# Start of a decoder layer on one core: x loaded by tokens with its squares summed along rows, the first unit's products in float32, and another order of the first two blocks

## The chip, the cores and the metric

One of the eight cores of a Trainium2 chip runs the whole layer. The metric is the device time of one execution in microseconds (us); lower is better. The engines are PE (TensorE, matmuls), ACT (ScalarE), DVE (VectorE), POOL (GpSimd) and SP (SyncE, which here only issues DMA transfers). Each takes its instructions in the order in which the program lists them.

## What is computed

A decoder layer over 256 tokens of width 2048, all in float32. Cut to the part that this case touches:

```python
mod = silu(c) @ w_ada[l] + b_ada[l]                       # 6 vectors of 2048: shifts, scales, gates
sh1, sc1, gt1, sh2, sc2, gt2 = split(mod, 6)
h = rmsnorm(x, g_pre_mix[l]) * (1.0 + sc1) + sh1          # x is 256 x 2048
proj = h @ w_in[l]                                        # q, k, v of two attentions, an indexer, two gates
# ... two attentions, gated merge, output projection, MLP of width 8192, residuals
```

## The kernel before

**Tiles.** Features are cut into KT = 16 blocks of P = 128, tokens into NT = 2 halves, the columns of `w_in` into chunks of CW = 512. `xt` holds x by features: `xt[:, k]` is block k, 128 features by 256 tokens.

**Products.** A float32 product is made of three faster ones. ACT casts a piece of the weight w to its high part wh (line 269, up to 1024 columns at a time), DVE subtracts it from w to get the low part wl (line 270), h is split in the same way, and PE adds hi·wh, hi·wl and lo·wh (lines 284 to 286). A *unit* is the work on one chunk of columns for a few blocks: `dk1[0:3]` is the second chunk of one attention's keys, blocks 0 to 2. Its two PSUM banks, one per token half, are ps0a and ps1a, or ps0b and ps1b in turn. When the unit ends they are *evicted* into an accumulator in SBUF such as `p_dk1`: by an ACT copy (line 527) the first time, by a DVE add (line 529) for ps0 later, while ps1 is refilled from the accumulator by a copy (line 315) ahead of its unit and copied out again.

**The sweep.** h of block k needs `sc[k]` and `sh[k]`, each the dot product of 128 rows of `w_ada` (1 MB) with silu(c): one DVE instruction over 2048 columns (`ada_item`, line 466). So the kernel sweeps over the blocks: the planner `sweep()` lists loads of `w_ada` ("sc k", "sh k") and units over the blocks that are there already, in an order from estimated loading and working times. `items` is that list; every item has a `load` (a DMA issue on SP into one of four buffers "w"), a `split` (casts and subtractions, or the dot) and perhaps an `mm` (products and evictions). The loop at the end of the program issues loads and splits some items ahead of the products; a scheduler then sets the order of ACT's and DVE's instructions, save where a stretch stands under `manual_schedule`, which keeps the order of the code. The first FIRST = 2 blocks come as "sc", "sh" and one unit `first_products` over four chunks (EARLY: two of the indexer's queries, mq0, mk0); their eight banks stay open over both blocks.

**The start.** `start()` loads silu's argument, the identity and xT in four transfers, makes `cB` (silu(c) along every partition), squares x by features and adds the squares over partitions with matmuls against a column of ones (`pss`), takes the root of the mean and spreads its inverse into `rx`, keeps PE busy with `keep_warm` (matmuls whose result nobody reads), and does the dots, h (`h_block`) and weight splits of block 0. In this kernel DVE alone is under manual order there.

## Time and profile before

| | |
|---|---|
| median of 3 runs | 1473.7 us (1473.13 to 1476.2) |
| the profiled execution's own time | 1474.31 us |
| its span in the profile | 1472.5 us |
| PE busy | 1449.0 us, 98% |
| DVE busy | 1049.1 us, 71% |
| ACT busy | 772.8 us, 52% |
| moved by DMA | 371.60 MB, mean 252 GB/s |

The span is what the profiler saw from first to last instruction; some 2 us lie around it. Busy shares are means over the whole span: whether an engine bounds a stretch is read from the waits of that stretch. The profile gives TensorE's granted clock as a share of full speed.

### The profile page before, as it was taken

To read this page: it belongs to the slowest core of one execution; us is meant where nothing else is said; L and a number is where in the kernel's file an instruction comes from. 1 tells how busy PE (TensorE), PEld (TensorE's weight loads), DVE (VectorE), ACT (ScalarE), POOL (GpSimd) and SP (SyncE) were. 2 spreads that over 40 slices of the span, in tenths; PEclk is the share of its full clock that TensorE was granted. 3 is DMA by queue.
4 is the path that set the end of the run, shared out by engine and by line. 5 is a ranking of instruction groups with operands and counts; after the bars stand their busy time and mean duration, and the time that the engine had idled before them with its cause. 6 is when DMAs were issued, how large, how long until landed. Compare 5 with 4: busy or idle time off the path is not lost.

```text
span 1472.5 us, 18227 instructions
## 1 busy us (share of the span) xinstructions
PE 1449.0 (98%) x7042; PEld 1214.0 (82%) x7042; DVE 1049.1 (71%) x1317; ACT 772.8 (52%) x1113; POOL 5.7 (0%) x14
## 2 busy tenths in 40 slices
PE   7999999999999999999999999999999999999997
PEld 6877788778888888888888888888888888888886
DVE  6799887999876777987587665677655655565555
ACT  4676776667685454444474444444434443344443
POOL 0000000000000000000000000000000000000000
PEclk9999999999999999999999999999999999999999
DMA  8999996475879899878526666756765545555551
GB/s 315 325 330 333 343 343 245 177 280 207 335 274 327 332 347 335 321 290 312 233 95 250 256 234 252 257 218 240 257 243 190 196 177 195 200 198 176 198 189 68
DMA packets 56150, 371.60 MB, mean 252 GB/s; under 512 B 6464, under 2 KB 6624, under 8 KB 15616
## 3 DMA queue, kind: packets, MB, share of 16 engines
q1 hardware_dynamic: 55152, 367.98, 68.3%
q0 software_dynamic: 704, 2.18, 0.5%
q8 instruction: 55, 0.90, 0.2%
q10 hardware_dynamic: 208, 0.28, 0.1%
q14 instruction: 31, 0.25, 0.1%
HBM read 368.30 MB, written 2.11 MB: 252 GB/s over the span
## 4 chain that ended last, share of the span: by engine, by line
PE 92%; DVE 4%; ACT 1%; issue 1%; DVEq 0%; ACTq 0%
PE ps L286 16%; PE ps L285 16%; PE ps L284 16%; PE ps L365 16%; PE ps L367 8%; PE ps0b L285 1%; PE ps0b L284 1%; PE ps0b L286 1%; PE ps1b L285 1%; PE ps0a L284 1%; PE ps1b L286 1%; PE ps0a L285 1%; DVE wl L270 1%; PE ps1b L284 1%; PE ps0a L286 1%; PE ps1a L286 1%
## 5 line engine op out<-in xcount | busy, mean ns | idle before, releaser
L270 DVE TENSOR_TENSOR wl<-w,wh 128x1024 fp32r<-128x1024 f32 (+1 forms) x472 | 562.7, 1202 | 333.4 <-ACT wh L269 324.8
L269 ACT CAST wh<-w 128x1024 fp32r<-128x1024 f32 (+1 forms) x472 | 486.8, 1035 | 552.5 <-PE ps L286 336.3
L365 PE MATMUL ps<-h,wh 128*128 128x512 f32 (+1 forms) x1056 | 257.1, 386 | 0.0
L466 DVE SCALAR_TENSOR_TENSOR w<-w,cB 128x2048 f32<-128x2048 f32 x96 | 219.3, 2285 | 29.5 <-DMA w<-in_ada 29.3
L365 PEld LDWEIGHTS ps<-h,wh 128*128 128x128 f32 x1056 | 186.8, 189 | 32.1
L284 PE MATMUL ps<-wh,f 128*128 128x512 f32 x512 | 199.3, 389 | 0.0
L285 PE MATMUL ps<-wl,f 128*128 128x512 f32 x512 | 199.2, 389 | 0.0
L286 PE MATMUL ps<-wh,f 128*128 128x512 f32 x512 | 199.2, 389 | 0.0
L367 PEld LDWEIGHTS ps<-h,wl 128*128 128x128 f32 x1024 | 139.5, 190 | 9.7
L367 PE MATMUL ps<-h,wl 128*128 128x256 f32 x1024 | 142.8, 282 | 0.0
L284 PE MATMUL ps<-wh,h 128*128 128x512 f32 x320 | 126.8, 396 | 0.0
L285 PE MATMUL ps<-wl,h 128*128 128x512 f32 x320 | 124.9, 390 | 0.0
L286 PE MATMUL ps<-wh,h 128*128 128x512 f32 x320 | 124.9, 390 | 0.0
L284 PEld LDWEIGHTS ps<-wh,f 128*128 128x128 f32 x512 | 96.1, 188 | 20.0
L286 PEld LDWEIGHTS ps<-wh,f 128*128 128x128 f32 x512 | 96.1, 188 | 20.0
L285 PEld LDWEIGHTS ps<-wl,f 128*128 128x128 f32 x512 | 96.1, 188 | 19.8
L286 PEld LDWEIGHTS ps<-wh,h 128*128 128x128 f32 x320 | 60.1, 188 | 12.7
L284 PEld LDWEIGHTS ps<-wh,h 128*128 128x128 f32 x320 | 60.1, 188 | 12.2 <-issue 0.3
L285 PEld LDWEIGHTS ps<-wl,h 128*128 128x128 f32 x320 | 60.2, 188 | 11.9
L284 PE MATMUL ps<-wh,o 128*128 128x512 f32 x128 | 50.1, 391 | 0.0
L286 PE MATMUL ps<-wh,o 128*128 128x512 f32 x128 | 49.8, 389 | 0.0
L285 PE MATMUL ps<-wl,o 128*128 128x512 f32 x128 | 49.8, 389 | 0.0
(326 smaller groups left out, 1791.6 us busy)
## 6 DMA issues: line engine op xcount, KB each, us to landing
w<-in_w_ff SPq DMA_DIRECT2D x128, 1024.0 KB, 4.8
w<-in_ada SPq DMA_DIRECT2D x96, 1024.0 KB, 6.0
w<-in_w_in SPq DMA_DIRECT2D x60, 1024.0 KB, 6.3
w<-in_w_in SPq DMA_DIRECT2D x27, 768.0 KB, 6.0
w<-in_w_o SPq DMA_DIRECT2D x16, 1024.0 KB, 5.7
w<-in_w_moba SPq DMA_DIRECT2D x8, 1024.0 KB, 7.1
w<-in_w_dsa SPq DMA_DIRECT2D x8, 1024.0 KB, 7.1
w<-in_w_in SPq DMA_DIRECT2D x14, 512.0 KB, 4.8
```

The lines of the kernel that those rows point to most:

```text
L269: yield (lambda h=h, src=src: S.copy(h, src), lambda h=h, l=l, src=src: V.tensor_tensor(l, src, h.bitcast(F32), ALU.subtract))
L270: lambda h=h, l=l, src=src: V.tensor_tensor(l, src, h.bitcast(F32), ALU.subtract))
L284: TE.matmul(ps[t][:, :cw], hi, h, start=f, stop=False, skip_group_check=skip)
L285: TE.matmul(ps[t][:, :cw], hi, l, start=False, stop=False, skip_group_check=skip)
L286: TE.matmul(ps[t][:, :cw], lo, h, start=False, stop=e, skip_group_check=skip)
L365: TE.matmul(out, w, acts()[:, k, :, ts], start=k == 0 and ts.start == 0, stop=False)
L367: TE.matmul(out[:, 0], w, acts()[:, k, 0, ts], start=False, stop=k == KT - 1)
L466: V.scalar_tensor_tensor(w, w, 1.0, cB, ALU.mult, ALU.mult, accum_out=mod[:, i:i + 1])
```

## The change

x comes in by tokens first (four transfers of 512 KB into the tile that held the squares), and ACT squares each part with a running sum along its row (`accum_out`), so that the sums over features come out directly; the DVE adds and the matmuls with ones are gone. cs and con are loaded from ACT's queue. xT is still needed and is loaded in pieces: blocks 0 and 1 in the start, blocks 2 and 3 after the first six items, then four blocks at a time, six items ahead of sh 4, sh 8 and sh 12. Unit 0's products are float32 matmuls of h (written over `xt[:, 0]`) with the raw weights, without cast or subtraction. The new `h_first` takes the place of `h_block` for blocks 0 and 1; block 1's high part is made before its float32 copy, and unit 1 goes hi·wh, lo·wh, hi·wl over its four chunks in the order 2, 3, 0, 1, with the evictions inside. One warm-up matmul more; all of `start()` is in manual order on ACT too and covers the first six items.

```diff
@@ -397,7 +397,7 @@
 
     xt = pre.tile([P, KT, T], F32, name="xt")
     spare = pre.tile([P, 4, 2 * CW], F32R, name="spare")
-    sq = act.tile([P, KT, T], F32, name="sq", tag="act")
+    sq = act.tile([P, NT * D], F32, name="sq", tag="act")
...
-        nc.sync.dma_start(cs[:, 0], cT)
-        nc.sync.dma_start(con[:, :P], consts[:, :P])
-        for h in range(4):
-            nc.sync.dma_start(xt[:, 4 * h:4 * h + 4], xT[:, 4 * h:4 * h + 4])
+        nc.scalar.dma_start(cs[:, 0], cT)
+        nc.scalar.dma_start(con[:, :P], consts[:, :P])
+        xs = [(t, h, sq[:, (2 * t + h) * D // 2:(2 * t + h + 1) * D // 2]) for t in range(NT) for h in range(2)]
+        for t, h, part in xs:
+            nc.sync.dma_start(part, x[t * P:(t + 1) * P, h * D // 2:(h + 1) * D // 2])
+        items[0]["load"]()
+        nc.sync.dma_start(xt[:, :FIRST], xT[:, :FIRST])
+        for it in items[1:4]:
+            it["load"]()
         nc.gpsimd.dma_start(b_sb, bT)
         nc.gpsimd.dma_start(g_sb, gT)
         S.activation(cs[:, 1], cs[:, 0], AF.Sigmoid)
         V.tensor_tensor(cs[:, 0], cs[:, 0], cs[:, 1], ALU.mult)
         sqrt_table(cs[:, 1, 0:1])
-        for n in range(NC):
-            S.copy(cB[:, n * CW:(n + 1) * CW], rows(cs[:, 0, 4 * n:4 * n + 4], ("tp", "sc")[n % 2]))
-        for it in items[:4]:
-            it["load"]()
-        pss = [bank(tag, "pss") for tag in ("tp", "sc")]
-        for h in range(4):
-            s4 = sq[:, 4 * h:4 * h + 4]
-            S.activation(s4, xt[:, 4 * h:4 * h + 4], AF.Square)
-            V.tensor_tensor(s4[:, 0:2], s4[:, 0:2], s4[:, 2:4], ALU.add)
-            if h == 3:
-                V.tensor_tensor(s4[:, 0:1], s4[:, 0:1], s4[:, 1:2], ALU.add)
-            n = 1 if h == 3 else 2
-            for i in range(n):
-                for t in range(NT):
-                    TE.matmul(pss[t][:, 0:1], s4[:, i, t * P:(t + 1) * P], ones[:, 0:1],
-                              start=h == 0 and i == 0, stop=h == 3)
         V.tensor_scalar(g_sb, g_sb, -0.5, None, ALU.mult)
         for sec in (1, 4):
             V.tensor_scalar(b_sb[:, sec * KT:(sec + 1) * KT], b_sb[:, sec * KT:(sec + 1) * KT], 1.0, None, ALU.add)
+        ssx = sm.tile([P, NT, 2], F32, name="ssx", tag="ssx", bufs=1)
+        for n, (t, h, part) in enumerate(xs):
+            S.copy(cB[:, n * CW:(n + 1) * CW], rows(cs[:, 0, 4 * n:4 * n + 4], ("tp", "sc")[n % 2]))
+            S.activation(part, part, AF.Square, accum_out=ssx[:, t, h:h + 1])
         a, rc, q, m = (sm.tile([P, NT], F32, name=f"x{i}", tag=f"x{i}", bufs=1) for i in "arqm")
-        items[0]["split"]()
-        for t in range(NT):
-            V.tensor_copy(m[:, t:t + 1], pss[t][:, 0:1])
-        root = rsqrt_mean(rc, a, m, q)
-        run(root)
+        V.tensor_tensor(m, ssx[:, :, 0], ssx[:, :, 1], ALU.add)
+        run(rsqrt_mean(rc, a, m, q))
         S.copy(rx, rows(rc, "sc")[:, :T])
-        keep_warm(rx, 4)
-        items[1]["split"]()
-        first = list(items[2]["halves"]())
-        h0 = h_block(0)
-        next(h0)
-        for high, low in first:
-            high()
-            low()
-        next(h0, None)
+        keep_warm(rx, 5)
+        for k in range(FIRST):
+            scale, shift, unit = items[3 * k:3 * k + 3]
+            if k:
+                shift["load"]()
+            scale["split"]()
+            h = h_first(k)
+            next(h)
+            if k:
+                unit["load"]()
+            shift["split"]()
+            next(h)
+            parts = list(unit["halves"]())[::-1] if k else ()
+            for high, _ in parts:
+                high()
+            next(h, None)
+            for _, low in parts:
+                low()
+            if not k:
+                unit["mm"]()
+                unit["mm"] = lambda: None
...
+    def h_first(k):
+
+        sc, sh = s1[:, 0, k:k + 1], s1[:, 1, k:k + 1]
+        i = KT + k
+        V.scalar_tensor_tensor(sc, mod[:, i:i + 1], b_sb[:, i:i + 1], g_sb[:, 0, k:k + 1], ALU.add, ALU.mult)
+        hf = tmpt("hf")[:, :T]
+        V.scalar_tensor_tensor(hf, xt[:, k], sc, rx, ALU.mult, ALU.mult)
+        yield
+        V.tensor_tensor(sh, mod[:, k:k + 1], b_sb[:, k:k + 1], ALU.add)
+        dst = xt[:, k], h1[:, k, 0]
+        S.activation(dst[k > 0], hf, AF.Identity, bias=sh)
+        yield
+        S.activation(dst[k == 0], hf, AF.Identity, bias=sh)
+        V.scalar_tensor_tensor(h1[:, k, 1], hf, sh, h1[:, k, 0].bitcast(F32), ALU.add, ALU.subtract)
+
     def h_block(k):
-
         sc, sh = s1[:, 0, k:k + 1], s1[:, 1, k:k + 1]
         i = KT + k
         V.scalar_tensor_tensor(sc, mod[:, i:i + 1], b_sb[:, i:i + 1], g_sb[:, 0, k:k + 1], ALU.add, ALU.mult)
@@ -493,7 +509,6 @@
         V.scalar_tensor_tensor(hf, xt[:, k], sc, rx, ALU.mult, ALU.mult)
         S.activation(h1[:, k, 0], hf, AF.Identity, bias=sh)
         V.scalar_tensor_tensor(h1[:, k, 1], hf, sh, h1[:, k, 0].bitcast(F32), ALU.add, ALU.subtract)
-        yield
         S.activation(xt[:, k], hf, AF.Identity, bias=sh)
...
     def first_products(off, k):
 
+
         it = {}
 
         def mm():
-            for i, name in enumerate(EARLY):
-                if k == 0:
+            if k == 0:
+                for i, name in enumerate(EARLY):
                     opened[name] = hold(name) if name in IQ else pair(True)
-                else:
-                    products(opened[name], h1, k, it["parts"][i:i + 1], CW, (), (), range(NT), True)
-                if k == FIRST - 1:
                     for t in range(NT):
-                        evict(name, True, False, t, opened[name][t])
-            for p, q in ((0, 0), (1, 0), (0, 1)) if k == 0 else ():
-                for i, name in enumerate(EARLY):
+                        TE.matmul(opened[name][t], xt[:, 0, t * P:(t + 1) * P], it["w"][:, i * CW:(i + 1) * CW],
+                                  start=True, stop=False, skip_group_check=True)
+                return
+            for p, q in ((0, 0), (1, 0), (0, 1)):
+                for i in (2, 3, 0, 1):
+                    name = EARLY[i]
                     for t in range(NT):
-                        TE.matmul(opened[name][t], h1[:, 0, p, t * P:(t + 1) * P], it["parts"][i][q],
-                                  start=p == q == 0, stop=False, skip_group_check=True)
-        it.update(load=lambda: load(it, w_in, off, 4 * CW), split=lambda: split(it, CW, 4),
+                        TE.matmul(opened[name][t], h1[:, k, p, t * P:(t + 1) * P], it["parts"][i][q],
+                                  start=False, stop=k == FIRST - 1 and q == 1, skip_group_check=True)
+                        if q:
+                            evict(name, True, False, t, opened[name][t])
+        it.update(load=lambda: load(it, w_in, off, 4 * CW), split=lambda: None,
                   halves=lambda: halves(it, CW, 4), mm=mm)
...
-            items.append(ada_item(0, k0, (lambda k=k0: run(h_block(k))) if k0 else None))
+            if k0 % 4 == 0 and k0:
+                items.insert(len(items) - 6, dict(load=lambda k=k0: nc.sync.dma_start(xt[:, k:k + 4], xT[:, k:k + 4]),
+                                                  split=lambda: None, mm=None))
+            items.append(ada_item(0, k0, (lambda k=k0: h_block(k)) if k0 >= FIRST else None))
...
-    items.insert(24, dict(load=lambda: nc.sync.dma_start(con[:, P:], consts[:, P:]), split=lambda: None, mm=None))
+    items.insert(3 * FIRST, dict(load=lambda: nc.sync.dma_start(xt[:, FIRST:4], xT[:, FIRST:4]), split=lambda: None, mm=None))
+    items.insert(26, dict(load=lambda: nc.sync.dma_start(con[:, P:], consts[:, P:]), split=lambda: None, mm=None))
...
-    with tc.manual_schedule(engines={mybir.EngineType.DVE}):
+    with tc.manual_schedule(engines={mybir.EngineType.DVE, mybir.EngineType.Activation}):
         start()
-    loads, splits = 4, 3
+    loads = splits = 3 * FIRST
```

The scheduler's order on ACT and DVE is another one from the start to some 180 rows of ACT further on; from there the two programs agree. Three places follow. Numbers behind names tell buffers of one name apart.

ACT around dk1[0:3], which runs right after dq1[0:3], before (spare and wh of w_440 are the casts of dk1[0:3]; p_dq1 is the eviction of the unit ahead of it; h1_90 and xt_81 are h of a block of features):

```order
L491 ACTIVATE s1_91<-mod_89,b_sb_85 128x1
L269 CAST spare_82<-w_440 128x1024
L494 ACTIVATE h1_90<-hf_475,s1_91 128x256
L497 ACTIVATE xt_81<-hf_475,s1_91 128x256
L269 CAST spare_82<-w_440 128x512
L269 CAST wh_508<-w_470 128x1024
L527 COPY p_dq1_100<-ps0b_244 128x512
L527 COPY p_dq1_100<-ps1b_245 128x512
```

and in the changed kernel, where dk1[0:3]'s weights are w_427:

```order
L507 ACTIVATE s1_91<-mod_89,b_sb_85 128x1
L510 ACTIVATE h1_90<-hf_432,s1_91 128x256
L512 ACTIVATE xt_81<-hf_432,s1_91 128x256
L542 COPY p_dq1_100<-ps0b_205 128x512
L269 CAST spare_82<-w_427 128x1024
L542 COPY p_dq1_100<-ps1b_206 128x512
L269 CAST spare_82<-w_427 128x512
L269 CAST wh_467<-w_437 128x1024
```

The eviction of dq1's first bank has moved ahead of dk1's first cast, and that of its second bank ahead of the second.

ACT around mq1[4:7], which runs right after mk0[4:7], before (wh of w_918 are mq1's casts, p_mk0<-ps1a the eviction of mk0's second bank):

```order
L527 COPY p_mq0_92<-ps1b_245 128x512
L315 COPY ps1b_245<-p_mq1_94 128x512
L269 CAST wh_959<-w_918 128x1024
L491 ACTIVATE s1_91<-mod_89,b_sb_85 128x1
L269 CAST wh_963<-w_918 128x512
L494 ACTIVATE h1_90<-hf_952,s1_91 128x256
L497 ACTIVATE xt_81<-hf_952,s1_91 128x256
L527 COPY p_mk0_93<-ps1a_243 128x512
```

and in the changed kernel, where the weights are w_905:

```order
L542 COPY p_mq0_92<-ps1b_206 128x512
L315 COPY ps1b_206<-p_mq1_94 128x512
L542 COPY p_mk0_93<-ps1a_204 128x512
L507 ACTIVATE s1_91<-mod_89,b_sb_85 128x1
L269 CAST wh_940<-w_905 128x1024
L510 ACTIVATE h1_90<-hf_912,s1_91 128x256
L512 ACTIVATE xt_81<-hf_912,s1_91 128x256
L269 CAST wh_944<-w_905 128x512
```

The eviction of mk0's second bank and s have moved ahead of mq1's first cast. In the same way ACT's eviction p_mk0<-ps0a now stands ahead of the first cast of mq1[7:11].

DVE around mq1[2:4], which runs right after mk0[2:4], before (spare<-w_592 is the subtraction of mq1[2:4], p_mk0 the add that evicts mk0's first bank; w,mod is the dot of a scale or shift):

```order
L270 TENSOR_TENSOR wl_574<-w_538,wh_573 128x1024
L466 SCALAR_TENSOR_TENSOR w_556,mod_89<-w_556,cB_87 128x2048
L529 TENSOR_TENSOR p_mq0_92<-ps0b_244,p_mq0_92 128x512
L270 TENSOR_TENSOR spare_82<-w_592,spare_82 128x1024
L495 SCALAR_TENSOR_TENSOR h1_90<-hf_597,s1_91,h1_90 128x256
L529 TENSOR_TENSOR p_mk0_93<-ps0a_242,p_mk0_93 128x512
```

and in the changed kernel, where the weights are w_551:

```order
L509 SCALAR_TENSOR_TENSOR hf_556<-xt_81,s1_91,rx_88 128x256
L270 TENSOR_TENSOR wl_533<-w_497,wh_532 128x1024
L544 TENSOR_TENSOR p_mq0_92<-ps0b_205,p_mq0_92 128x512
L468 SCALAR_TENSOR_TENSOR w_515,mod_89<-w_515,cB_87 128x2048
L544 TENSOR_TENSOR p_mk0_93<-ps0a_203,p_mk0_93 128x512
L270 TENSOR_TENSOR spare_82<-w_551,spare_82 128x1024
L511 SCALAR_TENSOR_TENSOR h1_90<-hf_556,s1_91,h1_90 128x256
```

The add of mk0's first bank has moved from behind the subtraction to ahead of it.

## Rows read from the trace of the kernel before

**Rows 1.** The page: the span, and section 1 (busy time, share of the span, instructions of each engine).

```profile
span 1472.5 us, 18227 instructions
PE 1449.0 (98%) x7042; PEld 1214.0 (82%) x7042; DVE 1049.1 (71%) x1317; ACT 772.8 (52%) x1113; POOL 5.7 (0%) x14
```

**Rows 2.** Table of stretches; columns: stretch in us, its length, then busy us (instructions) of PE, PEld, DVE, ACT and POOL, the granted clock of TensorE (1.00 is full speed), the DMA engines' share, GB/s.

```profile
30.00:35.00 5.00, 4.96 (x11) 3.47 (x12) 5.00 (x5) 2.73 (x3) 0.00 (x0) 0.50 0.67 228
60.00:240.00 180.00, 178.36 (x779) 145.14 (x778) 154.94 (x181) 125.78 (x203) 0.00 (x0) 1.00 0.93 333
200.00:400.00 200.00, 197.22 (x981) 160.54 (x980) 179.56 (x313) 131.65 (x236) 0.00 (x0) 1.00 0.70 257
```

**Rows 3.** The timeline of PE in its first 42 us; columns: start in us, length in us, engine, line, operation, out<-in, shape, count, and in brackets the idle time before and what ended it. A row with xN holds N matmuls in one block, and a float32 matmul stands in it twice.

```profile
17.48 3.78 PE L229 MATMUL warm<-rx 128*128 128x256 f32 x8 [0.46 <-ACT rx L446]
20.69 2.38 PE L588 MATMUL h_iq<-wh,h 128*128 128x512 f32 x5
29.94 1.22 PE L284 MATMUL h_iq<-wh,h 128*128 128x512 f32 x2 [2.52 <-ACT wh L269]
38.64 0.39 PE L284 MATMUL ps0b<-wh,h 128*128 128x512 f32 x1
41.36 0.39 PE L284 MATMUL ps0a<-wh,h 128*128 128x512 f32 x1
```

**Rows 4.** The timeline of SP's DMA issues, then ACT's and DVE's rows of the start (same columns).

```profile
0.74 0.39 SPq L412 DMA_DIRECT2D cs<-in_cT  x1
1.66 1.85 SPq L415 DMA_DIRECT2D xt<-in_xT  x4
4.00 0.20 ACT L234 ACTIVATE dummy<-cs 128x1 f32<-128x1 f32 x1
8.23 2.97 ACT L428 ACTIVATE sq<-xt 128x1024 f32<-128x1024 f32 x3
15.02 0.17 DVE L195 TENSOR_SCALAR xa<-xm 128x2 f32<-128x2 f32 x1
16.12 2.29 DVE L466 SCALAR_TENSOR_TENSOR w<-w,cB 128x2048 f32<-128x2048 f32 x1
18.33 0.22 DVE L490 SCALAR_TENSOR_TENSOR s<-mod,b_sb,g_sb 128x1 f32<-128x1 f32 x1
18.65 0.48 DVE L493 SCALAR_TENSOR_TENSOR hf<-xt,s,rx 128x256 f32<-128x256 f32 x1
17.05 0.37 ACT L446 COPY rx<-prow 128x256 f32<-128x256 f32 x1 [1.63 <-PE prow L221]
28.05 0.51 ACT L494 ACTIVATE h<-hf,s 128x256 fp32r<-128x256 f32 x1 [0.42 <-DVE hf L493]
28.46 0.49 ACT L497 ACTIVATE xt<-hf,s 128x256 f32<-128x256 f32 x1
```

**Rows 5.** Two answers: how long the four transfers into xt took from issue to landing, and the instructions of line 904 (count, then min/median/max ns).

```profile
DMA to landing us min/median/max: 4.2/5.5/6.7
L904 ACT ACTIVATION_READ_ACCUMULATOR junk<-ps x8: 193/194/194, 679.6 to 747.4; 128x1 f32 x8
```

**Rows 6.** The timelines of ACT and DVE at three places of the sweep, for the spacing of evictions and casts.

```profile
40.88 0.59 ACT L527 COPY p_mq<-ps0b 128x512 f32<-128x512 f32 x1 [0.89 <-PE ps0b L286]
41.56 0.59 ACT L527 COPY p_mq<-ps1b 128x512 f32<-128x512 f32 x1
46.32 0.59 ACT L527 COPY p_mv<-ps0b 128x512 f32<-128x512 f32 x1
46.81 0.63 ACT L269 CAST spare<-w 128x512 fp32r<-128x512 f32 x1
137.39 0.29 ACT L491 ACTIVATE s<-mod,b_sb 128x1 f32<-128x1 f32 x1
137.58 1.03 ACT L269 CAST wh<-w 128x1024 fp32r<-128x1024 f32 x1
138.65 1.23 DVE L270 TENSOR_TENSOR wl<-w,wh 128x1024 fp32r<-128x1024 f32 x1 [0.81 <-ACT wh L269]
```

**Rows 7.** The timeline of PE: one float32 matmul of 256 columns (the first row) and what follows it.

```profile
338.27 0.59 PE L720 MATMUL po<-pT,p_mv 128*128 128x256 f32 x2
338.70 0.38 PE L721 MATMUL po<-pT,p_mv 128*128 128x128 f32 x2
```

**Rows 8.** The waits of PE between 200 and 400 us, its longest row.

```profile
PE po L720 <- DVE o L724: 1.4, 1, 1.4
```

**Rows 9.** The waits of PE between 60 and 240 us: what waited, for what, us in total, times, longest; this is the whole list.

```profile
PE ps0b L285 <- DVE wl L270: 1.6, 2, 0.8
```

**Rows 10.** The timelines of PE and DVE around the first of these two waits.

```profile
122.24 0.69 DVE L529 TENSOR_TENSOR p_mk<-ps0a,p_mk 128x512 f32<-128x512 f32 x1 [1.18 <-PE ps0a L286]
122.72 0.39 PE L284 MATMUL ps0b<-wh,h 128*128 128x512 f32 x1
122.84 1.22 DVE L270 TENSOR_TENSOR wl<-w,wh 128x1024 fp32r<-128x1024 f32 x1
124.12 0.50 PE L285 MATMUL ps0b<-wl,h 128*128 128x512 f32 x1 [0.79 <-DVE wl L270]
```

**Rows 11.** The waits for DMA between 60 and 160 us, the longest rows (us in total, times, longest).

```profile
ACT wh L269 <- DMA w<-in_w_in: 3.8, 2, 3.1
DVE w L466 <- DMA w<-in_ada: 3.2, 2, 2.7
```


## Prediction

> **What bounds the kernel now.** I read the page first: PE is busy for 1449.0 of 1472.5 us [rows 1], so a change pays only where it starts PE's stream of products earlier or takes a gap out of it. Next the table of stretches: at full clock everywhere after 40 us, 0.50 between 30 and 35 us [rows 2]. From 60 to 240 us, in the sweep, PE is idle for only 1.64 of 180 us while the DMA engines stand at 0.93 [rows 2]: PE sets the time there, with transfers close behind. Then PE's timeline of the start: warm-up matmuls at 17.48, first products at 20.69, a gap of 2.52 us before 29.94 (the casts of the second unit), then 24 products that take 38.64 − 29.94 = 8.70 us, and mq1's first product at 38.64 [rows 3]. At full clock a product takes 0.227 us, 24 of them 5.44 (12 products of mq1[0:2] lie between 38.64 and 41.36 [rows 3]); the lower clock after the gap so costs 3.3 us. All products later than 38.64 are the same in both kernels, so the question is when that one starts now, and whether PE can keep that lead.
>
> **The start, step by step.** *x and its squares.* SP's first issue was at 0.74 and x's at 1.66, with 6.7 us to the last landing [rows 4, 5]; x is now issued first, so it lands by about 0.74 + 6.7 + 1.4 (three more issues of 0.46) = 8.9. On ACT two issues of 0.39 (the time that SP's row shows [rows 4]) now stand ahead of the sigmoid, part of them under the wait for cs; I take the table's dummy to end at 4.55 rather than 4.20. Then four times a copy of cB (0.49, [rows 6]: from 46.32 to 46.81), a square of 1024 (0.96; three took 2.97 [rows 4]) and a read of its accumulator (0.19 [rows 5]): 6.6 us, to 11.2. x's last landing at 8.9 is hidden by this chain. The five DVE adds and 14 matmuls with a column of ones fall away. DVE's xa, 15.02 before, comes at 11.4.
>
> *Scales and shifts.* From xa to the next dot were 1.10 us (15.02 to 16.12 [rows 4]): the dot of sc 0 starts at 12.5. Each dot holds DVE for 2.21 (16.12 to 18.33), s for 0.32 (18.33 to 18.65) [rows 4], hf for 0.40. So hf of block 0 starts at 15.05, the dot of sh 0 at 15.45, and ends at 17.66; ACT's xt follows at 17.9, 0.41 to the next (28.05 to 28.46 [rows 4]), and PE can start on raw weights at 18.45, without a cast: 2.24 earlier than 20.69. rx, at 17.05 before, comes at 13.8, and five warm-ups of 0.80 each (four took 20.69 − 17.48 [rows 3]) reach to 18.
>
> *Unit 0.* One float32 matmul of 256 columns took 0.43 (338.27 to 338.70 [rows 7]), so one of 512 is 0.86 and eight are 6.9: end at 25.35. The 24 products that it replaces took from 20.69 to 29.94 − 2.52 = 27.42 [rows 3], 6.7 us, so this edit saves nothing in PE's time by itself; what it saves is two casts and two subtractions ahead of PE. At the lower clock the eight would be twice as long, 13.8; before, PE worked from 17.48 on and its first five products, 20.69 to 23.07, were still slow [rows 3]; the warm-ups now begin 3.3 us earlier, so I expect the clock to rise near 19 and count 6.9, with 13.8 as the upper bound.
>
> *Unit 1* waits for DVE: h's low part of block 0, dot sc 1 (19.25 to 21.46), s and hf, dot sh 1 (22.2 to 24.4), then ACT's h (24.65) and one cast: 26.1. PE so waits for at most 0.8 us rather than 2.52; a gap of 1.4 us left the clock at 1.00 [rows 2, 8], so I count full speed: 26.1 + 5.44 = 31.55 for mq1's first product. **Lead: 38.64 − 31.55 = 7.1 us.** Its bounds: 38.64 − (18.45 + 13.8 + 5.44) = 0.9 if all of unit 0 runs at the lower clock, and 38.64 − (25.35 + 5.44) = 7.9 with no gap ahead of unit 1. I take 7.1, since the rows before have PE at full speed after 5 us of work.
>
> **What the new order gives back.** ACT and DVE run their instructions in the order written, and PE's lead moves nothing in that. In the old order two places of the sweep had DVE's eviction of one unit's first bank ahead of the subtraction wl which the next unit needs: at mq1[4:7] and dq1[6:9]. These are PE's only two waits from 60 to 240 us, 0.8 each [rows 9], near 123 and 153. At the first, the next unit's first product is at T = 122.72, the eviction at T − 0.48, wl at T + 0.12 for 1.22, and the first hi·wl at 124.12, where two products of 0.227 after T it could have stood at T + 0.45 [rows 10]: 0.95, and 0.1 for the longer matmul, 1.05 lost. Call this **B**. In the changed order this pattern stands in more places, and two worse forms are new:
> - **A**: ACT evicts the first bank ahead of the cast. Eviction at T − 0.48 (40.88 against 41.36 [rows 3, 6]), the cast 0.49 later (46.32 to 46.81), wl 1.07 after it (137.58 to 138.65), 1.23 long [rows 6]: hi·wl at T + 2.37 rather than T + 0.45. Lost 1.92 + 0.1 = **2.0**.
> - **C**: ACT evicts the second bank too, and s, ahead of the cast: second eviction at T + 0.20 (41.56), 0.49, s 0.19 (137.39 to 137.58 [rows 6]): cast at T + 0.88, hi·wl at T + 3.24: 2.8 + 0.1 = **2.9**.
>
> By the order rows dk1[0:3] is now an A (+2.0), mq1[2:4] a B (+1.05), mq1[4:7] a C where it was a B (+1.85), mq1[7:11] an A (+2.0); dq1[6:9] stays a B. Sum 6.9. From then on both orders agree on every engine. What is late next is PE itself, and nothing after it has slack that could win this back.
>
> **Transfers.** The four of x by tokens replace four of xT, but xT comes too: 256 KB in the start and 1.75 MB in the sweep. At 333 GB/s [rows 2] that is 5.5 us of transfer in a stretch with 0.07 × 180 = 12.6 us free. The longest waits for DMA from 60 to 160 us are on DVE and ACT, 2.7 and 3.1 us [rows 11], and PE waited there for none. I take 0.3 us (the load of mv1[0:2] comes just in time), between 0 and 5.5. con's load goes two items later in the same queue; what uses it comes after the sweep's first passes, and I count nothing.
>
> **Sum.** The profiled execution took 1474.31 us, 0.6 over the median of the runs, 1473.7. 1474.31 − 7.1 + 6.9 + 0.3 = 1474.4, which for the runs' median is 1473.8. A difference under 0.2%, 2.9 us, is about what runs of this kernel can't tell from none.
>
> **Rivals.** *R1, the lead is kept (faster).* If a late cast is not the last thing that PE waits for, only the B's cost something: 1.05 new, so 1473.7 − 7.1 + 1.05 + 0.3 = **1468.0**. For it: ACT is busy only 126 of 180 us [rows 2], and the weights wait in their buffers for longer than a cast takes. Against it: both old B's show as waits, and no unit with its cast and subtraction ahead of the evictions does [rows 9]; it needs casts that run ahead of an eviction written before them. The Trainium skill, Perfetto Trace Analysis, section Tensor Engine Instruction, says that ACT and DVE are strict FIFO while PE can only pull weight loads ahead; by that rule an eviction which waits for PE holds up the cast behind it in every execution, and R1 is left only through my reading of the order. Rows 10 agree for DVE; no row here shows it for ACT. Chance 0.2.
>
> *R2, the stall of C drops the clock (slower).* At mq1[4:7] PE would be idle for 1.9 us (cast from T + 0.88, 1.03 long), work 0.45, and be idle again for 0.9. A gap of 2.52 dropped it and cost 3.3 [rows 3]; one of 1.4 did not [rows 8]. These lie on either side, so: 1473.8 + 3.3 = **1477.1**, and it decides the sign if the two gaps act as one. The Trainium skill, TensorE: Matmul & The Clock Gate, section What's actually happening, says that the window over which the gate judges activity is free-running and not tied to the kernel's start; by that rule the same gap costs 3.3 us in one execution and nothing in another. One profile can't show that. Chance 0.18.
>
> *R3, transfers become the bound (slower).* Two or three of the pieces of xT, 1.6 us each (512 KB at 333 GB/s), fall in front of a weight that is just in time: +3.3, **1477.1**. For it: DMA share 0.93 [rows 2], four buffers only, and PE now asks earlier. Against: no PE wait for a transfer now. Chance 0.12.
>
> **Chances and range.** The forecast (lead given back within 2.9 us) has 0.5. Of R1 0.18 is faster by over 0.2%, of R2 and R3 together 0.2 slower by as much; 0.04 of the forecast spills to either side. Faster 0.22, same 0.54, slower 0.24. The forecast's own range is 1471 to 1476.5; reaching into R1 and over R2 and R3, 1469 to 1478.
>
> **What will show it.** x's issue at 0.74, PE's float32 products from 18.45, unit 1 from 26.1, mq1 at 31.5, no clock of 0.5 near 30. PE's waits on ACT and DVE: about 1.9 in sum near 54 (dk1), 0.8 near 72, 2.8 near 119, 0.8 near 150, 1.9 near 175; from there PE's timelines coincide within 1 us. It is wrong if these waits are missing, if the first float32 products run at the lower clock, or if PE waits for transfers.

## The result, and the profile after

| | before | after |
|---|---|---|
| median, beside each other on one chip (6 runs each) | 1475.57 us (1473.13 to 1476.51) | 1485.32 us (1485.12 to 1487.97) |
| ratio, 95% interval | | 1.0073 (1.0062 to 1.0084) |
| the profiled execution's own time, its span | 1474.31, 1472.5 us | 1487.97, 1486.2 us |
| moved by DMA | 371.60 MB | 373.70 MB |

The changed kernel is slower, by 9.75 us of the medians; 1473.8, practically the time of before, had been forecast, with a range up to 1478. The profiled execution of after is the slowest of its six, 2.65 over the median, and that of before 1.26 under its median here: the two profiles lie 13.7 us apart, 3.9 more than the medians. All positions below are those of the profiled executions.

The page of after, against [rows 1]:

```profile
span 1486.2 us, 18155 instructions
PE 1451.4 (98%) x7008; PEld 1202.8 (81%) x7008; DVE 1046.5 (70%) x1311; ACT 770.2 (52%) x1113; POOL 5.7 (0%) x14
```

PE has 34 matmuls fewer on record and is busy for 2.4 us more. Idle time alone doesn't explain that.

**The start.** The table of stretches of after (columns as in [rows 2]):

```profile
20.00:30.00 10.00, 9.00 (x22) 4.10 (x21) 7.86 (x13) 2.91 (x5) 0.00 (x0) 0.95 0.77 273
30.00:35.00 5.00, 5.00 (x23) 3.95 (x23) 4.22 (x4) 4.02 (x7) 0.00 (x0) 1.00 0.94 362
60.00:240.00 180.00, 173.15 (x736) 138.46 (x737) 149.03 (x172) 120.09 (x192) 0.00 (x0) 0.99 0.90 327
```

As forecast, the clock of 0.50 between 30 and 35 us is gone. From 60 to 240 us PE is now idle for 6.85 us rather than 1.64. PE's timeline of the start (as [rows 3]):

```profile
6.91 3.65 PE L221 MATMUL prow<-con,cs 128*128 128x128 f32 x16 [6.91 <-DMA con<-in_consts]
21.71 3.70 PE L597 MATMUL h_iq<-w,xt 128*128 128x512 f32 x8 [0.35 <-ACT xt L498]
27.82 1.02 PE L597 MATMUL ps1a<-w,xt 128*128 128x512 f32 x2
29.49 0.50 PE L604 MATMUL ps0b<-wh,h 128*128 128x512 f32 x1 [0.65 <-ACT wh L269]
35.15 0.39 PE L284 MATMUL ps0b<-wh,h 128*128 128x512 f32 x1
```

and the issues of SP and ACT, then ACT's and DVE's rows (as [rows 4]):

```profile
0.74 2.06 SPq L416 DMA_DIRECT2D sq<-in_x  x4
0.74 0.41 ACTq L412 DMA_DIRECT2D cs<-in_cT  x1
5.29 0.22 ACT L423 ACTIVATE cs<-cs 128x16 f32<-128x16 f32 x1 [2.35 <-DMA cs<-in_cT]
8.04 0.59 ACT L431 COPY cB<-prow 128x512 f32<-128x512 f32 x1 [1.01 <-PE prow L221]
9.57 0.58 ACT L431 COPY cB<-prow 128x512 f32<-128x512 f32 x1
14.46 0.17 DVE L195 TENSOR_SCALAR xa<-xm 128x2 f32<-128x2 f32 x1
15.57 2.29 DVE L468 SCALAR_TENSOR_TENSOR w<-w,cB 128x2048 f32<-128x2048 f32 x1
```

mq1's first product starts at 35.15, against 38.64 [rows 3]: a lead of 3.49 us, half of the forecast's. Two rows show where the delay begins: ACT's at 5.29, a wait of 2.35 us for cs, which was issued at 0.74, and PE's first at 6.91, which waits for con. The transfers of this start (KB each, median us from issue to landing), in after, and then the rows of cs and con in before:

```profile
sq<-in_x SPq DMA_DIRECT2D x4, 512.0 KB, 6.2
cs<-in_cT ACTq DMA_DIRECT2D x1, 8.0 KB, 4.5
con<-in_consts ACTq DMA_DIRECT2D x1, 64.0 KB, 5.6
```

```profile
cs<-in_cT SPq DMA_DIRECT2D x1, 8.0 KB, 1.7
con<-in_consts SPq DMA_DIRECT2D x1, 64.0 KB, 2.1
```

The 8 KB of cs, issued at the same moment as x, take 2.8 us longer than when they were first, and the 64 KB of con 3.5 us longer. The first copy of cB needs both: the table's dummy on ACT, late through cs, ends at 7.02, and the copy then waits 1.01 us more for PE's rows, late through con.

**The sweep.** PE's waits from 60 to 240 us, the whole list (before: one line, [rows 9]):

```profile
PE ps0b L284 <- ACT wh L269: 2.7, 2, 1.8
PE ps0b L285 <- DVE wl L270: 2.0, 4, 0.8
PE ps0a L284 <- ACT spare L269: 0.9, 1, 0.9
PE ps0b L285 <- DVE spare L270: 0.9, 1, 0.9
PE ps0a L285 <- DVE spare L270: 0.5, 1, 0.5
```

The longest, at mq1[4:7], in the timelines of ACT and PE, and then two stretches of 2 us from the table of stretches:

```profile
124.04 0.59 ACT L542 COPY p_mk<-ps1a 128x512 f32<-128x512 f32 x1 [2.98 <-PE ps1a L286]
124.72 1.03 ACT L269 CAST wh<-w 128x1024 fp32r<-128x1024 f32 x1
125.81 0.50 PE L284 MATMUL ps0b<-wh,h 128*128 128x512 f32 x1 [1.80 <-ACT wh L269]
127.07 0.80 PE L285 MATMUL ps0b<-wl,h 128*128 128x512 f32 x1 [0.53 <-DVE wl L270]
127.66 0.63 PE L286 MATMUL ps0b<-wh,h 128*128 128x512 f32 x1
128.09 0.63 PE L285 MATMUL ps1b<-wl,h 128*128 128x512 f32 x1
```

```profile
126.00:128.00 2.00, 1.47 (x4) 0.94 (x4) 2.00 (x3) 2.00 (x5) 0.00 (x0) 0.71 0.38 135
128.00:130.00 2.00, 2.00 (x6) 1.52 (x5) 1.84 (x3) 2.00 (x5) 0.00 (x0) 0.50 0.54 150
```

ACT stood idle for 2.98 us before an eviction, with the cast two places behind it (s stands between them). By the trace the weights of that cast had landed at 122.01, so for 2.0 of these 2.98 us it lacked only its turn. After the two gaps PE's products follow each other in 0.43 us (127.66 to 128.09), at a granted clock of 0.50, the level of 1.2 GHz.

**Where PE does not wait.** From 560 to 760 us PE is busy for 198.52 of 200 us before (a wait of 1.2 us near the end, which in after comes behind 760) and for all 200 after, mostly in products of the same operands. In the rows `o` is the attentions' output, `y` the gated merge, `h2` the MLP's input, `f` its hidden layer, and `more` are split weights. The groups of that stretch by form, before and then after (count, busy us, mean ns of one):

```profile
L284 PE MATMUL ps<-wh,o 128*128 128x512 f32 x128 | 50.1, 391 | 0.0
L284 PE MATMUL ps<-wh,y 128*128 128x512 f32 x112 | 43.8, 391 | 0.0
```

```profile
L284 PE MATMUL ps<-wh,o 128*128 128x512 f32 x128 | 50.9, 397 | 0.0
L284 PE MATMUL ps<-wh,y 128*128 128x512 f32 x112 | 43.8, 391 | 0.0
```

Products with `o` got longer, those with `y` did not. In the timeline of PE, before and then after, one row and the eighth product behind it:

```profile
609.53 0.39 PE L284 MATMUL ps<-wh,o 128*128 128x512 f32 x1
611.34 0.39 PE L286 MATMUL ps<-wh,o 128*128 128x512 f32 x1
```

```profile
620.53 0.40 PE L285 MATMUL ps<-wl,o 128*128 128x512 f32 x1
622.39 0.40 PE L284 MATMUL ps<-wh,o 128*128 128x512 f32 x1
```

1.81 us became 1.86. Over all such pairs without a wait a product with `o` comes 0.2268 us after the last one before and 0.2333 after; 384 of them make 2.5 us. What differs is their place in memory: in the built program the new tile `ssx` takes 32 bytes of each partition, and every tile allocated behind it stands 32 bytes further. xt, o, h2 and more (the same place in turn) go from byte 196,480 to 196,512, spare from 212,864 to 212,896. y and f share a place ahead of it, at byte 84,864, and did not move.

How the two programs drift apart, from the starts of the same product in both (after minus before, us); the last column says what lies between a row and the one above it, in us:

| product at, before | offset | what lies between |
|---|---|---|
| 38.64 | -3.49 | the start |
| 60 | -2.15 | casts of mv1[0:2] and dq0: 1.34 |
| 62 | -0.01 | dk1[0:3]: 2.14 |
| 77 | +1.07 | mq1[2:4]: 1.08 |
| 133 | +4.50 | mq1[4:7]: 2.0 of waits, 1.3 of clock |
| 177 | +6.92 | mq1[7:11]: 2.1 |
| 300 | +7.95 | slow drift |
| 340 | +9.56 | a wait of 1.18 at 335 us |
| 560 | +9.57 | nothing |
| 735 | +12.26 | products with `o`: 2.5, with `more` 0.2 |
| 1460 | +14.05 | the MLP, products with `h2`: 1.8 |

### The profile page after: what moved, and what is told of

It is laid out like the page before. It is cut to its first block, busy times and chain, and to the rows that moved or that the text cites. A ratio compares the mean times of both kernels' runs of the same rounds, so it can differ in the third digit from the quotient of the medians.

```text
span 1486.2 us, 18155 instructions
## 1 busy us (share of the span) xinstructions
PE 1451.4 (98%) x7008; PEld 1202.8 (81%) x7008; DVE 1046.5 (70%) x1311; ACT 770.2 (52%) x1113; POOL 5.7 (0%) x14
## 2 busy tenths in 40 slices
DMA packets 56870, 373.70 MB, mean 251 GB/s; under 512 B 6544, under 2 KB 6704, under 8 KB 16336
## 4 chain that ended last, share of the span: by engine, by line
PE 88%; DVE 5%; ACT 3%; DMA 2%; issue 1%; DVEq 0%; ACTq 0%
PE ps L286 16%; PE ps L285 16%; PE ps L284 16%; PE ps L365 16%; PE ps L367 8%; DVE w L468 2%; DVE wl L270 1%; DMA w<-in_ada 1%; PE ps0b L285 1%; ACT wh L269 1%; PE ps0b L286 1%; PE ps0a L284 1%; PE ps0a L285 1%; PE ps0b L284 1%; PE ps1b L285 1%
## 5 line engine op out<-in xcount | busy, mean ns | idle before, releaser
L365 PE MATMUL ps<-h,wh 128*128 128x512 f32 (+1 forms) x1056 | 260.2, 388 | 0.0
```

The costliest lines, as they stand in the source:

```text
L365: TE.matmul(out, w, acts()[:, k, :, ts], start=k == 0 and ts.start == 0, stop=False)
```

## The experiments

Theory 1 is the start: the lead is short because cs and con land late. Theory 2 is the order: PE's waits in the sweep come from evictions that stand ahead of casts and subtractions. Theory 3, of addresses, was formed on the spacing above: the 32 bytes slow products all over the kernel. Its rival was that the drift is some other effect of the changed code, such as the transfers. Each time is compared with runs of before on the same chip: medians of 1475.99, 1474.76 and 1474.53 us in the three groups (e1 to e4, e5 to e8, e9 to e12).

### e1_cs_first: cs and con ahead of x

```diff
-        nc.scalar.dma_start(cs[:, 0], cT)
-        nc.scalar.dma_start(con[:, :P], consts[:, :P])
+        nc.sync.dma_start(cs[:, 0], cT)
+        nc.sync.dma_start(con[:, :P], consts[:, :P])
```

> The changed kernel with one thing put back: cs and the identity part of con are issued on SP ahead of x's four transfers, as in the kernel before. Theory 1 (the small transfer cs queues behind x's 2 MB, so ACT's sigmoid starts at 5.29 rather than 2.47 us): sigmoid again near 2.5, the copies of cB start near 5, mq1's first product at 32 to 33 rather than 35.15, and the kernel is 2.5 to 3 us faster than the changed one, about 1482.5 us. Rival (the start is bound by x's landing or by the float32 products): mq1's first product stays near 35 and the time near 1485.

1485.23 us (1484.25 to 1487.45), ratio 1.0072 (1.0057 to 1.0087): no gain that can be told from after. ACT and PE in its start:

```profile
2.34 0.22 ACT L423 ACTIVATE cs<-cs 128x16 f32<-128x16 f32 x1 [0.32 <-DMA cs<-in_cT]
6.12 1.06 ACT L432 ACTIVATE sq<-sq 128x1024 f32<-128x1024 f32 x1 [1.03 <-DMA sq<-in_x]
19.86 3.70 PE L597 MATMUL h_iq<-w,xt 128*128 128x512 f32 x8
28.59 0.50 PE L604 MATMUL ps0b<-wh,h 128*128 128x512 f32 x1 [1.60 <-ACT wh L269]
```

cs is there 2.95 us earlier and unit 0 starts 1.85 earlier, but now the squares wait for x, and the dot of sc 1 waits 0.86 us for its weights at 21.58. Unit 1 gains 0.90, mq1 0.96 (34.19). So late cs and con are the first limit in the start and the transfers themselves are the next, close behind it: theory 1 names the delay rightly, and putting them back ahead buys far less than the 2.5 to 3 us expected. In its profiled execution e1 is 2.2 us ahead of after at 300 us and loses 1.8 of them by 560, where PE waits 1.76 and 1.01 us (at 334 and 498) on subtractions behind dots that waited for w_ada.

### e2_casts_first, e3_both, e4_before_casts_first: an order for the whole sweep

ACT and DVE are put under manual order over the whole sweep and items are split until two units stand ready ahead of the one that runs, in after (e2), after with e1's edit (e3) and the kernel before (e4):

```diff
-        while splits < min(len(items), i + (1 if it.get("alone") else 2 + deep)):
+        while splits < min(len(items), i + (1 if it.get("alone") else 2 + deep)) or (
+                i < SWEEP_END - 8 and splits < loads and sum(x["mm"] is not None for x in items[i + 1:splits]) < 2):
...
+    with tc.manual_schedule(engines={mybir.EngineType.DVE, mybir.EngineType.Activation}):
+        for i in range(2, SWEEP_END):
+            loads, splits = turn_of(i, loads, splits)
```

> The changed kernel with ACT and DVE in the order of the code over the whole sweep, and splits issued until two units with products (not two items of any kind) are split ahead, so that every cast and subtraction stands ahead of the evictions of the unit before it. Theory 2 (evictions that wait for PE hold up the casts behind them): PE's waits for ACT and DVE at dk1[0:3], mq1[2:4], mq1[4:7] and mq1[7:11], and the drop of the clock behind mq1[4:7], go; 7 to 9 us faster than the changed kernel, 1476 to 1478 us. Rival (the pieces of xT starve the sweep): the waits stay or turn into waits for DMA, under 2 us faster.

> Both edits together. If theories 1 and 2 hold and add up, 10 to 12 us faster than the changed kernel, 1473 to 1475.5 us, and no more than 1 us of PE wait between 40 and 240 us. If the loads of the sweep set the time once PE runs earlier, the two do not add up: 1476 to 1478 us, with waits that end with DMA.

> The kernel before, with the same rule of order as in e2_casts_first alone. It has two waits of 1.05 us of this kind, so theory 2 gives 1 to 2 us faster than before, about 1473.5 us; if the rule of order has costs or gains of its own, apart from those waits, it moves by more than that either way, and e2 and e3 have to be read against this one.

e2: 1509.21 us, ratio 1.0233 (1.0218 to 1.0249). e3: 1507.44, 1.0219 (1.0204 to 1.0234). e4: 1503.27, 1.0188 (1.0165 to 1.0211). The order by itself costs the kernel before 27 us. The waits of PE in e4 from 60 to 240 us, the longest:

```profile
PE ps1a L284 <- ACT ps1a L315: 5.3, 5, 2.2
PE ps0b L284 <- ACT ps0b L315: 3.7, 1, 3.7
```

With the casts far ahead, it is the refills of the PSUM banks (line 315) that stand too far back, and PE waits for those. By 240 us the profiled execution of e4 is 15 us behind that of before; it loses as much again by 340, with waits for DVE and a granted clock of 0.95 between 240 and 420 us, which weren't followed up. The edit was too broad and says nothing on theory 2, except that casts ahead of everything isn't the cure.

### e5_pad: the new tile 64 bytes wide

```diff
-        ssx = sm.tile([P, NT, 2], F32, name="ssx", tag="ssx", bufs=1)
+        ssx = sm.tile([P, 4 * NT, 2], F32, name="ssx", tag="ssx", bufs=1)[:, :NT]
```

> The changed kernel with the new tile ssx made 64 bytes wide on each partition instead of 32; the order of instructions is the same on every engine. In the changed kernel the 32 bytes push every tile that is placed after it (xt, spare, o, h2) from an address that is a multiple of 64 to one that is not, and the products that read spare or o follow each other in 0.2333 us rather than 0.2267. Theory 3 (the shifted address slows those products): 0.2267 everywhere again, 5 to 6.5 us faster than the changed kernel, 1479 to 1480.5 us. Rival (the slower products come from this execution's clock or from contention with the extra transfers): spacing and time as in the changed kernel, 1485.

1479.67 us (1478.19 to 1480.53), ratio 1.0032 (1.0019 to 1.0045): 4.8 us better than after, each against its own runs of before, by bytes that nobody reads or writes. But it isn't a return to the old spacing: products with `o` stay at 0.233 us, those reading `spare` fall from 0.2334 only to 0.2298 (before 0.2273), and the MLP runs faster than before, its offset falling from +10.51 at 735 us to +6.22 at 1460. PE's wait at 335 us is also missing from its profiled execution. So the spacings, in which no wait has a part, say that the time of a product hangs on its operand's address, but not by a simple rule of 64 bytes.

### e6_before_shifted: the kernel before, with a tile of 16 bytes that nobody reads

```diff
+        G.memset(sm.tile([P, 4], F32, name="unused", tag="unused", bufs=1), 0.0)
```

The tile takes 32 bytes in the built program, as `ssx` does.

> The kernel before with nothing but an unused tile of 32 bytes per partition in the same pool, cleared once by POOL. Theory 3: products that read spare, o or h2 at 0.2333 us, 5 to 6.5 us slower than before, 1480 to 1482 us. Rival: no change, 1475.5.

1480.26 us (1479.0 to 1481.78), ratio 1.0034 (1.0022 to 1.0047): 5.5 us slower than before, with nothing changed but one memset on POOL and addresses. In its profile the offset against before grows as the theory has it: +1.26 at 300 us, +2.47 between 560 and 661 (`o`), +1.78 in the MLP; and a wait of 1.15 at 328.50 for DVE, as after has one at 335. Products with `o`, `spare` and `more` come 0.2333, 0.2335 and 0.2334 us apart. The group of products with `o`, as above:

```profile
L284 PE MATMUL ps<-wh,o 128*128 128x512 f32 x128 | 50.9, 398 | 0.0
```

This settles that the shift alone slows the kernel before, by some 5.5 us; that after pays about as much for it is tested in e9.

### e7_pad_casts_first: e5, with the order mended at five places

At dk1[0:3], mq1[2:4], mq1[4:7], mq1[7:11] and dq0 the older unit's evictions are put behind the next unit's casts (ACT) or its first subtraction (DVE), by an edge that orders the issue and adds no wait (FIVE_PLACES stands for the list of these pairs of units; the lines that fill `evicted` and `unit_of` are left out):

```diff
+    for older, unit, ts in FIVE_PLACES:
+        for t in ts:
+            kind, out = evicted[older, t]
+            tc.add_manual_dep(out.ins, unit_of[unit][kind][-1 if kind == "casts" else 0].ins.name, issue_only, reason="order")
```

> As e5_pad, with ACT and DVE told for five places alone to issue an eviction behind the casts and subtractions of the unit that follows it: dq1[0:3] before dk1[0:3], mk0 before mq1 at blocks 2, 4 and 7, mv0[0:2] before dq0[0:3]. Theory 2 (these evictions hold up the casts): the waits of PE at those units go and with them the lower clock behind mq1[4:7], together some 9 us in the trace; 6 to 9 us faster than e5_pad, 1471 to 1474 us. Rival (PE waits for weights that have not landed, whatever the order): under 2 us faster than e5_pad.

1473.84 us (1472.02 to 1476.25), ratio 0.9996 (0.9987 to 1.0006): 5.8 us better than e5. ACT and PE at mq1[4:7]:

```profile
122.31 1.03 ACT L269 CAST wh<-w 128x1024 fp32r<-128x1024 f32 x1
124.56 0.57 ACT L545 COPY p_mk<-ps1a 128x512 f32<-128x512 f32 x1
123.39 0.50 PE L285 MATMUL ps0b<-wh,h 128*128 128x512 f32 x1 [0.40 <-ACT wh L269]
124.65 0.50 PE L286 MATMUL ps0b<-wl,h 128*128 128x512 f32 x1 [0.53 <-DVE wl L271]
```

The cast has moved ahead of the eviction, PE waits 0.40 for it rather than 1.80, and the clock stays at 1.00. The waits at mq1[7:11] are gone. Not all is: 0.53 is left at dk1, and mq1[2:4] now waits 0.69 and 0.53 (0.85 in after). By the offsets against before, e7 wins back 3.0 us of e5's losses at mq1[4:7] (more than half of it clock), 1.9 at mq1[7:11], 0.9 at dk1 and 0.7 ahead of dk1, and loses 0.6 more at mq1[2:4]. Theory 2 holds for the two that matter most: in after the weights of mq1[4:7] and mq1[7:11] had landed 2.7 and 3.7 us before their casts began, and moving the evictions alone took the waits away at the second and cut the first's from 1.80 to 0.40 us. At dk1 transfers have a part:

```profile
58.46 1.57 ACT L269 CAST spare<-w 128x1024 fp32r<-128x1024 f32 x2
```

is its cast in e7, and by the trace its weights land at 58.44. With the order mended the weights are the limit there, and dk1 still loses 1.3 us against before, where they landed at 56.47 and the cast began at 58.56. At mq1[2:4] the cast in e7 stands behind the rows of h (74.12 to 75.26), while its weights land at 74.77.

### e8_all: e7 with e1's edit and a sixth place

The edits of e7 and e1 together, and the same edge at dq1[6:9].

> As e7_pad_casts_first, with cs and con issued on SP ahead of x as in e1_cs_first, and the same rule at dq1[6:9], where the kernel before waits too. If the three causes add up: 1 us from the start and 1 from dq1 on top of e7, 1469 to 1472 us, faster than the kernel before by 3 to 6 us. If transfers bound the sweep once PE leads by 5 us: as e7 or slower, with waits that end with DMA.

1472.52 us (1470.97 to 1474.11), ratio 0.9985 (0.9976 to 0.9994): 2.2 us faster than before, and 1.3 better than e7 by the medians, though the intervals of the two overlap. By the offsets at 300 us it is 1.5, of which dq1[6:9] has 0.4 and the earlier start the rest: as far as these two executions show, the lead that e1 lost again is kept here, where the order no longer eats it.

### e9_sums_in_mod: after, with the addresses of before

```diff
-        ssx = sm.tile([P, NT, 2], F32, name="ssx", tag="ssx", bufs=1)
+        ssx = mod[:, 5 * KT:5 * KT + 2 * NT].rearrange("p (t h) -> p t h", h=2)
```

The sums lie in four columns of `mod` that aren't in use yet, and no tile moves.

> The changed kernel with ssx kept in four columns of the existing tile mod, so that every tile lies where it lies in the kernel before (e5_pad moved them by 64 bytes, and there spare was read at 0.230, o still at 0.2333, h2 faster than before). Theory 3, as e5_pad and e6_before_shifted leave it (the time of a product depends on where its operand lies, in steps finer than 64 bytes): 0.2267 for spare, more and o again, the first-layer products of the MLP as before, together 2.7 us in the sweep, 3 between 560 and 760 us and 1.9 in the MLP: 1478 to 1479.5 us. Rival: the spacing follows something else in the changed kernel, and stays at 0.2333 for o.

1480.66 us (1479.17 to 1484.69), ratio 1.0048 (1.0032 to 1.0063). Spacings are those of before again (`o` 0.2268, `spare` 0.2271, `more` 0.2267), and the offset of +6.27 at 340 us is +6.26 at 1460: nothing is lost behind the sweep. By medians that is 3.6 us better than after, each against its own runs of before, less than e6's 5.5 but with an interval of 2.3 us on either side. What is left, 6.1 us, is the waits less the lead of 3.53. It shows one thing more, PE's two waits at mq1[4:7] in its timeline, and the stretch around the second (length, PE's busy time, granted clock, DMA share, GB/s):

```profile
124.79 0.50 PE L284 MATMUL ps0b<-wh,h 128*128 128x512 f32 x1 [1.80 <-ACT wh L269]
126.05 0.50 PE L285 MATMUL ps0b<-wl,h 128*128 128x512 f32 x1 [0.52 <-DVE wl L270]
```

```profile
126.00:128.00 2.00, 1.95 (x9) 1.00 0.19 57
```

The same gaps as in after, 1.80 and 0.52 us, and the clock stays at 1.00.

### e10_all_in_mod and e11_h2_moved: the best of it

e10 is e8 with the sums in `mod`; e11 is e10 with `h2` alone moved 64 bytes on, where e5 had found the MLP to be fast:

```diff
+        if pool is not act:
+            whole = pool.tile([P, KT * 2 * T + 16], F32R, name=name, tag="act")
+            n = 16 if name == "h2" else 0
+            return whole[:, n:n + KT * 2 * T].rearrange("p (k s t) -> p k s t", s=2, t=T)
```

> As e8_all, with ssx in mod as in e9_sums_in_mod instead of 64 bytes wide. By the spacings of e8: 1.2 us won in the sweep and 2.4 in the products with o, 3.8 lost in the MLP, where h2 at 64 bytes off was faster: within 1 us of e8_all, 1471.5 to 1473.5 us.

> As e10_all_in_mod, with h2 alone moved by 64 bytes, to where e5, e7 and e8 had it. If the address of h2 is what made the MLP faster there: 3.5 to 4.5 us faster than e10_all_in_mod, 1467.5 to 1469.5 us, and faster than the kernel before by 5 us or more. If it was another tile or something else: as e10_all_in_mod.

e10: 1473.27 us (1472.12 to 1474.51), ratio 0.9993 (0.9984 to 1.0002). e11: 1469.73 us (1468.63 to 1470.9), ratio 0.9970 (0.9958 to 0.9982), 4.8 us faster than before and the fastest of all. The offset of e11 goes from -0.63 at 735 us to -5.04 at 1460; that of e10 stays (+0.47, +0.46). So the larger part of the gain over before is an address again, and it has nothing to do with the change.

### e12_unit0_split: e9 with unit 0 in split products

```diff
-                        TE.matmul(opened[name][t], xt[:, 0, t * P:(t + 1) * P], it["w"][:, i * CW:(i + 1) * CW],
-                                  start=True, stop=False, skip_group_check=True)
-                return
...
-            parts = list(unit["halves"]())[::-1] if k else ()
+            parts = list(unit["halves"]())[::-1]
```

> As e9_sums_in_mod, with unit 0 in three products of split weights again (24 instead of eight float32 ones), in the order of unit 1. Its two casts and subtractions come back ahead of the dot of sc 1 on DVE: the first unit's products start 1 us later than 21.7, unit 1 and mq1 start 2 to 3 us later than in the changed kernel (29.5 and 35.15), so 2 to 3 us slower than e9_sums_in_mod if the start alone counts. If the later stalls take up a later start, as they took up the earlier one: under 1 us slower.

1485.04 us (1484.09 to 1487.04), ratio 1.0075 (1.0061 to 1.0089): 4.4 us slower than e9, more than the 2 to 3 expected. PE's row at the start of unit 1, and a stretch (columns as in e9's):

```profile
31.71 0.80 PE L600 MATMUL ps0b<-wh,h 128*128 128x512 f32 x1 [3.50 <-ACT wh L269]
```

```profile
30.00:35.00 5.00, 3.29 (x8) 0.55 0.65 223
```

Without the float32 products the casts of unit 0 delay those of unit 1, PE is idle for 3.50 us and then runs slow until about 37 us; mq1 starts at 39.88 rather than 35.11. The float32 unit is worth 4.8 us there, not by its own length (6.97 us of PE, against 6.57 for the 24 products of before) but because it leaves ACT and DVE to unit 1.

## Why the prediction was wrong

The forecast had after 0.1 us over before, and 9.75 were measured. Addresses make some 5.5 of that by e6 and 3.6 by e9, the lead came 3.6 short, and the rest lies in the waits and the clock of the sweep.

**The step that failed most: "All products later than 38.64 are the same in both kernels".** The program is the same there, its time is not. One tile of 32 bytes moved the operands of products all over the kernel, at 2.7 to 2.9% each for `spare`, `o` and `more`. Undone in after it gave 3.6 us (e9, with an interval of 2.3 on either side), done to before it took 5.5 (e6). No term of the sum and no rival stood for it; nothing in the trace of before could have priced it, but that a tile was added ahead of others could be seen in the diff.

**The lead: 3.49 us, not 7.1.** The term "I take the table's dummy to end at 4.55 rather than 4.20" priced the move of cs and con by its two issues alone, with no term for their landing beside x, and left out that the copies of cB wait for con as well. The sigmoid came at 5.29 rather than at 2.47 as before and the dummy ended at 7.02; PE's rows began when con had landed, at 6.91, against 3.38 in before, and with that the first copy of cB, forecast for about 4.6, came at 8.04. From there the chain is as forecast: four times 1.53 us (8.04 to 9.57) against 1.64, the dot of sc 0 1.11 behind xa, float32 products of 6.97 us against 6.9, 0.65 of waiting ahead of unit 1 where "at most 0.8" was said. The dot of sc 0 was 3.07 late, and unit 1 3.39. The Trainium skill, DMA: Bandwidth & Descriptors, section Issuing engines are not separate DMA queues, says that transfers issued by different engines run on the same 16 DMA engines and interleave; the row of cs agrees, 4.5 us from ACT's queue beside x, 1.7 when first. The clock's part was right: float32 at full speed (0.429 us for each half of a product from 22.2 us on), and no 0.50 near 30 us.

**What the order gives back: right in kind, and in size but for the clock.** dk1[0:3] was forecast at 2.0 and lost 2.14; mq1[2:4] 1.05 and 1.08; mq1[7:11] 2.0 and 2.1; mq1[4:7] 1.85 and 2.0 by its waits. The two ahead of dk1 were missed: mv1[0:2] and dq0, 1.34 together, small waits for a subtraction that a late transfer (1.0 us) or evictions had put off. e7 confirms the cause in the main: 5.8 us came back by moving evictions at five places. For dk1 and mq1[2:4] the close agreement is in part luck: e7 left 1.3 of dk1's loss, to weights that land late, and did not reduce mq1[2:4]'s.

**R1 (the lead is kept) fell.** The rows of before [rows 10] had shown only for DVE that a piece of work behind an eviction waits with it. In after ACT shows it, idle for 2.98 us with the cast behind the eviction of p_mk at 124.04, as the rule of the Trainium skill that stood beside R1 (Perfetto Trace Analysis, section Tensor Engine Instruction) has it.

**R2 (C drops the clock) came true in part.** Products ran at 0.50 from 127 to 130 us, which cost 1.3 us and not 3.3, since the clock came back after seven products; at 30 us in before, where the 3.3 was read, thirteen had run slow. The Trainium skill, TensorE: Matmul & The Clock Gate, section What's actually happening, has the window in which activity is judged run freely; by that rule the same gaps need not do the same, and the runs agree: 1.80 and 0.52 or 0.53 us dropped the clock in after, e1, e5 and e12, and not in e9. Why it stayed up in e9 is not shown beyond that.

**R3 (transfers) had a small part.** In the rows around PE's waits from 60 to 240 us the cast or subtraction stands behind an eviction. At dk1 alone a transfer is close behind: its weights land at 58.78 in after, 0.85 us before the cast and 2.3 later than in before; a piece of xT was issued ahead of them at 48.54, but no run takes it out. A wait of 1.18 at 335 us does go back to a transfer, by a dot that waited 1.50 for w_ada. It comes and goes: none in e5, e8, e10 and e11; 1.15 in e6, 1.31 in e7, 1.76 in e1, 1.68 in e9. As e6 has the transfers of before, the pieces of xT are not needed for it.

**The sum of after**, by its profile: -3.49 (start), +1.34 and +7.3 (waits of the order), +1.3 (clock), +1.4 (335 us), +2.5 and +0.2 and +1.8 (`o`, `more`, MLP), and the drift in the sweep, 1.6 as e6 has between 38 and 300 us: 14.0, against 14.05 at 1460 us and 13.7 of the spans. In the medians it is 9.75. Which of these terms the other executions were spared stays open, as one execution is profiled; the clock and the wait at 335 us are the ones that were seen to come and go. As an estimate, 13.7 less these two (2.7) and less the 1.26 by which before's profiled execution lies under its median is 9.7.

## To carry to other kernels

A new tile, however small, can move every tile behind it; where PE is the bound, compare the spacing of the same products far from the change before explaining a difference by the change, and pad or place small tiles so that nothing moves. A short transfer that heads a chain is better issued ahead of large ones; a queue of its own, on ACT, did not spare it the wait here. A lead on PE is kept only if the orders of ACT and DVE give it room: evictions of the unit that runs go behind the casts and subtractions of the next one, but not so far behind that the refill of a bank is late.

## What the runs showed of the hardware that was not expected

Starts of one 512-column product after another at full clock, without a wait, by the operand's distance from its place in before (mean us over 40 to 300 us or over 560 to 760 us, between two products that both read the operand):

| operand | 0 bytes | 32 bytes | 64 bytes |
|---|---|---|---|
| `spare` (weights, sweep) | 0.2271 (e9), 0.2273 | 0.2334 (after), 0.2335 (e6) | 0.2298 (e5) |
| `more` (weights) | 0.2267 | 0.2334 | 0.2296 (e5) |
| `o` (tokens, 560 to 760) | 0.2268 | 0.2333 | 0.2334 (e5) |
| MLP with `h2` in all, against before | +0.0 us (e10) | +1.8 (after, e6) | -4.3 (e5), -4.4 (e11) |

Why an address does that, and why 64 bytes are good for `h2` and bad for `o`, the runs don't tell; other distances weren't tried. Products with `f` and `y`, whose place does not move, show the same mean length in all of these kernels, within 2 ns.
